# ScalarE's first Silu ahead of its bias loads, in the start of a hybrid attention and convolution layer

## Chip, core and metric

The kernel runs on one core of a Trainium2 chip. The metric is device time in microseconds, the median of several executions. One execution was also taken with the hardware profiler; all rows below are from it.

## What is computed

One layer of a diffusion model with two parallel head groups, in float32. The condition vectors go through Silu and a modulation matrix; the tokens are normalised, scaled and shifted by that, and projected. All the rest (attention, convolution, gates, output) follows from the projections.

```python
mod = jax.nn.silu(c) @ w_mod[l] + b_mod[l]           # c: (1, 1024), w_mod: (1024, 3072)
shift, scale, gate = jnp.split(mod, 3, axis=-1)
mod_c = jax.nn.silu(c_ctx) @ w_mod[l] + b_mod[l]     # the same for the context tokens
u = rms_norm(h, norm_w[l]) * (1.0 + scale[:, None, :]) + shift[:, None, :]   # h: (1, 1024, 1024)
p = u @ w_in[l]                                      # q, k, v, gates, GLU input
...
out = jnp.concatenate([attn, conv], axis=-1) @ w_out[l]
h = h + gate[:, None, :] * out
```

The small vectors that the change moves are `b_mod`, `norm_w`, `conv_b`, `conv_ln_w`, `conv_ln_b` and `b_pw`: together 40 rows of 128 numbers, 20 KB.

## The kernel before

The kernel has three stages: a start and the projections, the attention with the convolution beside it, and the output. Only the start matters here. Most operands of matmuls are split into a rounded high part and a remainder (`split`, L110 to L117), and products are taken of the parts.

`setup` (L139) comes first. It loads the two condition vectors as 16 rows of 128 into `crow` (half by SP, half by ACT) and the six bias vectors as 40 rows into `brow` (all by ACT, L147 to L150). GpSimd makes the identity matrix. TensorE turns `crow` into columns (`pc`, L160), ScalarE takes Silu of that (`sc`, L162), which needs a table load first. TensorE turns `brow` into columns too (`pb`, L169), and VectorE copies these to `bcol` and `vcol` (L171 to L175).

`start` (L949) then runs the steps listed in the string `START`, whose beginning is

```python
"L0 X0 L1 Q0 C0 W0 X1 Q1 L2 Y D0 Q2 R2 R0 L3 L4 Q3 R3 S0 | R1 C1 P00 P10 U00 W1 Q5 D1 M00 ..."
```

- `L` j (`mod_load`, L236): SP loads 256 columns of `w_mod` in four loads of 256 KB, two for each of two tiles; `wm` for j up to 2 (four buffers of the pool `e5`), `wm3s` and on after that.
- `X` h (`load_tokens`, L318): SP loads four token tiles of 512 KB.
- `Q` i (`norm_stats`, L326): ScalarE squares token tile i and sums, VectorE and GpSimd make the factor `rs`. `R` i (`scale`, L968) applies it to the tile on VectorE.
- `C` j (`mod_mm`, L256): TensorE multiplies `sc` with block j of `w_mod` (L265, tile `mrow`). For the first three blocks that is 8 products of full float32, which the trace shows as 16 matmuls.
- `D` j (`mod_cols`, L269): the result is copied out (`mrs`), turned into columns (`mcol`), and `bcol` is added (`modc`).
- `W` h, `S` h: SP loads half of the first projection weight (`wglu0s`), ScalarE and VectorE split it.
- `P` (`turn_x`, L341): transposes of the tokens (`xt`). `U` (`make_u`, L347): ScalarE applies `modc`. `M` (L965): the projection's matmuls (L387).

What sets the order: each engine executes its own queue in order, and a queue of loads is part of the engine that issues them (SP or ACT). The steps ahead of the bar in `START` keep the order written (`manual_schedule`). Everything else in `setup`, `start` and `project` is placed by a planner at build time: by priority in the order of the source, among the instructions that its own model of time has ready. It may put later work into gaps, also between hand-ordered steps. All semaphores are placed by the planner's framework. From the attention on, the order is written by hand again.

Of the kernel before, what the change touches and what calls it, by code (L numbers as in the profile page):

```python
# [12 lines left out]
AF = mybir.ActivationFunctionType  # L13
# [5 lines left out]
P = 128  # L19
# [62 lines left out]
class Layer:  # L82
# [56 lines left out]
    def setup(self):  # L139

        nc, a, cst = self.nc, self.a, self.cst
        row = lambda ap, n: ap.rearrange("o (r f) -> (o r) f", f=P)[0:n]
        crow = self.w2([16, P], "crow")
        brow = self.w2([40, P], "brow")
        nc.sync.dma_start(out=crow[0:8], in_=row(a["c"], 8))
        nc.scalar.dma_start(out=crow[8:16], in_=a["c_ctx"].rearrange("(r f) -> r f", f=P))
        nc.scalar.dma_start(out=brow[0:16], in_=row(a["b_mod"], 16))  # L147
        nc.scalar.dma_start(out=brow[16:24], in_=row(a["norm_w"], 8))
        for i, n in enumerate(("conv_b", "conv_ln_w", "conv_ln_b", "b_pw")):
            nc.scalar.dma_start(out=brow[24 + 4 * i:28 + 4 * i], in_=row(a[n], 4))  # L150
        self.ident = ident = cst.tile([P, P], F32, name="ident")
        make_identity(nc, ident)
        self.identr = cst.tile([P, P], F32R, name="identr")
        nc.vector.tensor_copy(out=self.identr, in_=ident)
        self.mhalf = cst.tile([P, 16], F32, name="mhalf")
        nc.gpsimd.memset(self.mhalf, -0.5)
        self.ones = cst.tile([P, P], F32, name="ones")
        nc.gpsimd.memset(self.ones, 1.0)
        pc = self.bank("t", "pc")
        nc.tensor.transpose(out=pc[:, 0:16], in_=crow, identity=ident[0:16, 0:16])  # L160
        self.sc = sc = cst.tile([P, 16], F32, name="sc")
        nc.scalar.activation(sc, pc[:, 0:16], AF.Silu)  # L162
        self.chl = chl = cst.tile([P, NK, 4], F32R, name="chl")
        cv = chl.rearrange("p k (s w) -> p w s k", w=2)
        scv = sc.rearrange("p (s k) -> p s k", s=2)
        nc.vector.tensor_copy(out=cv[:, 0], in_=scv)
        nc.vector.tensor_sub(out=cv[:, 1], in0=scv, in1=cv[:, 0].bitcast(F32))
        pb = self.bank("t", "pb")
        nc.tensor.transpose(out=pb[:, 0:40], in_=brow, identity=ident[0:40, 0:40])  # L169
        self.bcol = bcol = cst.tile([P, 24], F32, name="bcol")  # L170
        nc.vector.tensor_copy(out=bcol[:, 0:8], in_=pb[:, 0:8])  # L171
        nc.vector.tensor_scalar(out=bcol[:, 8:16], in0=pb[:, 8:16], scalar1=1.0, scalar2=None, op0=ALU.add)
        nc.vector.tensor_copy(out=bcol[:, 16:24], in_=pb[:, 16:24])
        self.vcol = cst.tile([P, 16], F32, name="vcol")
        nc.vector.tensor_copy(out=self.vcol, in_=pb[:, 24:40])  # L175
        self.modc = cst.tile([P, NK, 4], F32, name="modc")
# [897 lines left out]
```

## Time and profile before

| | us |
|---|---|
| median of 3 runs (675.5 to 676.73) | 676.3 |
| the profiled execution | 675.49 |
| its span on the core | 673.7 |
| around the span | 1.8 |

Busy time in the span: PE (matmuls) 646.5 us, 96%; DVE (VectorE) 518.5, 77%; ACT (ScalarE) 350.1, 52%; POOL (GpSimd) 347.7, 52%. The page cuts the span into 40 slices of 16.8 us: PE is busy for 4 tenths of the first, 8 of the second and 9 or more of nearly all that follow; the DMA engines are at 8 tenths and then 9 or more in the first three, and lower after that. So the first 50 us differ from the rest, and the change lies in the first 6.

How to read the rows: times are microseconds from the start of the span. In a timeline a row is start, duration, engine, line, operation, output and inputs, and in brackets the engine's idle time before it and what ended that. SPq and ACTq are the queues on which SP and ACT issue loads; an issue's duration there isn't the transfer's. Releasers are inferred from semaphores; where a wait is put down to something long done, it was another. Ends of matmuls are modelled.

### The profile page before, as it was taken

Reading aid. Unit: us, or ns where it says so; the run is one execution under the profiler, and the core shown is the slowest. Engines: PE = TensorE matmul, PEld = TensorE weight load, DVE = VectorE, ACT = ScalarE, POOL = GpSimd, SP = SyncE. Lnnn points to the kernel's source line nnn. Section 1 sums busy time; section 2 is a strip of 40 time slices with the busy share of each in tenths; the row PEclk is TensorE's granted clock in tenths of the full one; section 3 lists DMA queues with packets and bytes.
Section 4 is the critical chain, followed back from the end, with each engine's and each line's share of the span. In section 5 each row is a group of like instructions: output and inputs, shape, how many; then the busy total and the mean of one; then the engine's idle time right before and its main releaser. Section 6 shows DMA issues by size and latency. Waiting matters only on the chain.

```text
span 673.7 us, 11083 instructions
## 1 busy us (share of the span) xinstructions
PE 646.5 (96%) x4258; PEld 572.8 (85%) x4258; DVE 518.5 (77%) x828; ACT 350.1 (52%) x578; POOL 347.7 (52%) x305
## 2 busy tenths in 40 slices
PE   4899999999999999998999999999999999998997
PEld 1467799888888999998899999999999888987885
DVE  2698789959999999976888888888899856555322
ACT  3564325546343122134888888888888836431000
POOL 1243813966509343796575676887787854211100
PEclk9899999999999999999999999999999999999999
DMA  8994320312652314010010001001100022125611
GB/s 267 315 239 122 101 61 1 95 31 63 218 188 95 94 63 126 1 32 1 1 33 1 1 32 33 32 14 51 32 1 1 1 94 77 64 79 175 231 48 47
DMA packets 51253, 53.29 MB, mean 79 GB/s; under 512 B 4522, under 2 KB 41698, under 8 KB 51201
## 3 DMA queue, kind: packets, MB, share of 16 engines
q1 hardware_dynamic: 51104, 52.57, 25.1%
q8 instruction: 33, 0.54, 0.3%
q14 instruction: 20, 0.16, 0.1%
q10 hardware_dynamic: 96, 0.02, 0.0%
HBM read 44.20 MB, written 8.39 MB: 78 GB/s over the span
## 4 chain that ended last, share of the span: by engine, by line
PE 76%; DVE 15%; DMA 3%; issue 2%; ACT 2%; SPq 1%; DVEq 0%; ACTq 0%
PE o L824 13%; PE pv L719 11%; PE s L641 10%; PE pt L686 10%; DVE y L457 6%; PE g L387 6%; PE a L387 6%; PE kv L413 4%; DVE yp L457 4%; PE q L413 4%; PE zc L387 3%; PE pw L534 3%; PE mrow L265 1%; DMA wm3s<-in_w_mod 1%; DMA wglu0s<-in_w_in 1%
## 5 line engine op out<-in xcount | busy, mean ns | idle before, releaser
L710 POOL TENSOR_TENSOR p<-raw,p 128x512 fp32r<-128x512 f32 x96 | 128.1, 1349 | 64.0 <-DVE p L704 42.2
L641 PE MATMUL s<-kT,qT 128*128 128x512 f32 (+1 forms) x384 | 100.7, 372 | 3.4 <-ACT e L676 3.4
L719 PE MATMUL pv<-p,v 128*128 128x256 f32 x640 | 103.4, 292 | 0.4 <-DVE mm L751 0.2
L457 DVE SCALAR_TENSOR_TENSOR yp<-up,cw,yp 128x1024 f32<-128x1024 f32 x77 | 99.1, 1286 | 1.9
L686 PE MATMUL pt<-ident,e 128*128 128x128 f32 x640 | 93.4, 273 | 0.4 <-ACT raw L695 0.4
L719 PEld LDWEIGHTS pv<-p,v 128*128 128x128 f32 x640 | 86.0, 189 | 4.5 <-DVE mm L751 1.1
L676 ACT ACTIVATE e<-s,nm 128x1280 f32<-128x1280 f32 x64 | 84.9, 1326 | 2.9 <-DVE mj L666 2.9
L659 DVE TENSOR_REDUCE nm<-s 128x1 f32<-128x1024 f32 x64 | 78.0, 1219 | 5.6 <-PE s L641 4.9
L686 PEld LDWEIGHTS pt<-ident,e 128*128 128x128 f32 x640 | 73.5, 141 | 1.5 <-ACT raw L695 1.0
L641 PEld LDWEIGHTS s<-kT,qT 128*128 128x128 f32 x384 | 62.7, 189 | 9.8 <-ACT e L676 3.9
L695 ACT ACTIVATE raw<-pt 128x512 f32<-128x512 f32 x96 | 57.3, 598 | 12.6 <-PE pt L686 8.6
L666 DVE TENSOR_SCALAR_CACHE_REDUCE mj<-s,nm 128x256 bf16<-128x256 f32 x64 | 30.9, 483 | 20.2 <-PE s L641 18.2
L702 ACT ACTIVATE p<-pt 128x512 fp32r<-128x512 f32 x64 | 38.5, 601 | 12.7 <-PE pt L686 11.2
L704 DVE CAST p<-raw 128x512 fp32r<-128x512 f32 x96 | 41.7, 460 | 1.7 <-ACT raw L695 1.2
L710 DVE TENSOR_TENSOR p<-pt,p 128x512 fp32r<-128x512 f32 x64 | 41.2, 681 | 1.6 <-ACT p L702 1.6
L457 DVE SCALAR_TENSOR_TENSOR y<-up,cw,y 128x1024 f32<-128x1024 f32 x25 | 40.7, 1630 | 0.8
L837 DVE TENSOR_TENSOR r<-o,gb 128x512 f32<-128x512 f32 (+1 forms) x17 | 10.8, 655 | 36.1 <-PE o L824 36.1
L442 POOL TENSOR_TENSOR yz<-yz,ct 128x512 f32<-128x512 f32 x24 | 33.1, 1421 | 0.0
L124 POOL TENSOR_TENSOR qr<-qr,mhalf 128x8 f32<-128x8 f32 (+1 forms) x13 | 21.6, 1660 | 7.8 <-DVE qr L123 7.6
L117 POOL TENSOR_TENSOR ul<-u,uh 128x512 fp32r<-128x512 f32 x8 | 12.2, 1528 | 20.8 <-DVE uh L115 14.2
L441 ACT ACTIVATE ct<-up,cw 128x512 f32<-128x512 f32 x24 | 15.7, 714 | 12.8 <-DVE up L425 9.9
L625 ACT ACTIVATE za<-za 128x512 f32<-128x512 f32 x8 | 4.8, 596 | 29.1 <-PE za L413 29.1
(578 smaller groups left out, 1758.4 us busy)
## 6 DMA issues: line engine op xcount, KB each, us to landing
x<-in_x SPq DMA_DIRECT2D x8, 512.0 KB, 5.7
wg<-in_w_mod SPq DMA_DIRECT2D x8, 512.0 KB, 4.2
xr<-in_x SPq DMA_DIRECT2D x8, 512.0 KB, 6.1
out<-r SPq DMA_DIRECT2D x15, 256.0 KB, 2.0
wm<-in_w_mod SPq DMA_DIRECT2D x12, 256.0 KB, 6.6
zc_d<-zc SPq DMA_DIRECT2D x4, 512.0 KB, 3.3
za_d<-za SPq DMA_DIRECT2D x4, 512.0 KB, 4.0
zar<-za_d SPq DMA_DIRECT2D x4, 512.0 KB
```

The source lines that it names most:

```text
L387: nc.tensor.matmul(acc[h], lhsT=ww, rhs=uu[k][:, h * 512:(h + 1) * 512], start=first and i == 0, stop=last and i == 2)
L413: self.nc.tensor.matmul(acc[:, t * 256:(t + 1) * 256], lhsT=x, rhs=y, start=k == 0 and i == 0, stop=k == NK - 1 and i == 2)
L457: nc.vector.scalar_tensor_tensor(out=out, in0=up[:, w:w + S], scalar=cw[:, w:w + 1], in1=y if w else st["y2"], op0=ALU.mult, op1=ALU.add)
L641: mm = nc.tensor.matmul(self.s5[:, s0 + k0:s0 + k0 + n], lhsT=qt[:, h % 4, t * P:(t + 1) * P], rhs=kT[:, w, k0:k0 + n], start=w == 0, stop ...
L659: r = self.nc.vector.reduce_max(out=nm[:, 0:1], in_=self.s5[:, 1536 * t:1536 * t + 1024], axis=AX.X, negate=True)
L676: ex = nc.scalar.activation(e, self.s5[:, t * KEYS:(t + 1) * KEYS], AF.Exp, bias=st["nm", t][:, 1:2], accum_out=st["z"][:, t:t + 1])
L686: nc.tensor.transpose(out=tp[:, i * 256 + t * P:i * 256 + (t + 1) * P], in_=st["e", t][:, (2 * k + i) * P:(2 * k + i + 1) * P], identity=s ...
L695: self.nc.scalar.activation(raw, st["T", k], AF.Copy)
L704: nc.vector.tensor_copy(out=st["p", k][:, 0], in_=st["T", k])
L710: eng.tensor_sub(out=p[:, 1], in0=st["T", k], in1=p[:, 0].bitcast(F32))
L719: nc.tensor.matmul(st["pv"][:, 0:256], lhsT=self.v[:, kt, u[1] // 4].rearrange("p w d -> p (w d)"), rhs=st["p", k][:, j, i * 256:(i + 1) * ...
L824: self.nc.tensor.matmul(o, lhsT=p, rhs=q, start=half == k == i == 0, stop=half == 1 and k == 3 and i == 2)
```

## The change

In `setup`, ScalarE now takes Silu of a column of ones before anything else that it computes, and Silu of the condition vectors after that. The six loads of bias rows, which ACT issued first, stand in the source behind that second Silu. The result of the first Silu isn't used.

```diff
         nc.sync.dma_start(out=crow[0:8], in_=row(a["c"], 8))
         nc.scalar.dma_start(out=crow[8:16], in_=a["c_ctx"].rearrange("(r f) -> r f", f=P))
-        nc.scalar.dma_start(out=brow[0:16], in_=row(a["b_mod"], 16))
-        nc.scalar.dma_start(out=brow[16:24], in_=row(a["norm_w"], 8))
-        for i, n in enumerate(("conv_b", "conv_ln_w", "conv_ln_b", "b_pw")):
-            nc.scalar.dma_start(out=brow[24 + 4 * i:28 + 4 * i], in_=row(a[n], 4))
+        one = self.small([P, 1], "sj", "sj")
+        nc.vector.memset(one, 1.0)
+        nc.scalar.activation(one, one, AF.Silu)
         self.ident = ident = cst.tile([P, P], F32, name="ident")
...
         nc.scalar.activation(sc, pc[:, 0:16], AF.Silu)
+        nc.scalar.dma_start(out=brow[0:16], in_=row(a["b_mod"], 16))
+        nc.scalar.dma_start(out=brow[16:24], in_=row(a["norm_w"], 8))
+        for i, n in enumerate(("conv_b", "conv_ln_w", "conv_ln_b", "b_pw")):
+            nc.scalar.dma_start(out=brow[24 + 4 * i:28 + 4 * i], in_=row(a[n], 4))
```

## Rows read from the trace of the kernel before

**Rows 1.** The page, chain that ended last: shares of the span by engine.
```profile
PE 76%; DVE 15%; DMA 3%; issue 2%; ACT 2%; SPq 1%; DVEq 0%; ACTq 0%
```

**Rows 2.** The same chain in its first 36 us: start, duration, what.
```profile
1.20 3.13 DMA wm<-in_w_mod
...
4.34 5.50 DMA x<-in_x
...
11.30 6.95 DMA wglu0s<-in_w_in
...
24.21 7.19 DMA wm3s<-in_w_mod
...
31.42 1.07 ACT wm30h L113
...
34.39 2.14 DVE wm31l L117
```

**Rows 3.** Timeline of ACT and its queue, 0 to 20 us.
```profile
1.35 0.33 ACTq L147 DMA_DIRECT2D brow<-in_b_mod  x1
...
2.56 0.26 ACTq L150 DMA_DIRECT2D brow<-in_conv_ln_w  x1
3.75 0.26 ACTq L150 DMA_DIRECT2D brow<-in_conv_ln_b  x1
...
4.59 1.28 ACT L162 ACT_TABLE_LOAD   x1 [4.59 <-DMA brow<-in_norm_w]
5.88 0.18 ACT L162 ACTIVATE sc<-pc 128x16 f32<-128x16 f32 x1
9.87 1.06 ACT L330 ACTIVATE junk<-x 128x1024 bf16<-128x1024 f32 x1 [3.81 <-DMA x<-in_x]
...
13.81 1.06 ACT L330 ACTIVATE junk<-x 128x1024 bf16<-128x1024 f32 x1 [0.23 <-DMA x<-in_x]
```

**Rows 4.** Timeline of PE, 0 to 30 us.
```profile
2.67 0.25 PE L160 MATMUL pc<-ident,crow 16*128 16x16 f32 x1 [2.67 <-DMA crow<-in_c]
6.12 5.56 PE L265 MATMUL mrow<-wm,sc 128*2 128x256 f32 x16 [3.19 <-ACT sc L162]
11.61 0.25 PE L169 MATMUL pb<-ident,brow 40*128 40x40 f32 x1
...
15.72 5.30 PE L265 MATMUL mrow<-wm,sc 128*2 128x256 f32 x16 [0.84 <-DMA wm<-in_w_mod]
20.95 1.09 PE L344 MATMUL xt<-ident,x 128*128 128x128 f32 x8
...
26.22 3.66 PE L265 MATMUL mrow<-wm,sc 128*2 128x256 f32 x16 [0.95 <-DMA wm<-in_w_mod]
```

**Rows 5.** Waits of SP's queue, 4 to 6 us (sum, times, longest), and its second x issue.
```profile
SPq L322 <- DMA wm<-in_w_mod: 1.6, 2, 1.1
...
5.19 0.34 SPq L322 DMA_DIRECT2D x<-in_x  x1
```

**Rows 6.** Windows: busy us by engine (instructions), granted clock, DMA share, GB/s.
```profile
2.00:3.00 1.00, 0.25 (x1) 0.18 (x1) 0.00 (x0) 0.00 (x0) 0.00 (x0) 1.00 0.34 90
6.00:7.00 1.00, 0.88 (x3) 0.29 (x4) 0.37 (x2) 0.06 (x1) 0.00 (x0) 1.00 0.78 262
9.00:9.50 0.50, 0.50 (x3) 0.14 (x2) 0.00 (x0) 0.00 (x0) 0.00 (x0) 1.00 0.65 238
14.00:31.00 17.00, 13.85 (x61) 6.64 (x62) 10.77 (x28) 7.62 (x13) 4.52 (x14) 0.90 1.11 317
```

**Rows 7.** Timeline of DVE, 0 to 24 us.
```profile
1.49 0.23 DVE L154 CAST identr<-ident 128x128 fp32r<-128x128 f32 x1 [1.49 <-POOL ident masks.py:199]
...
13.17 0.75 DVE L969 TENSOR_SCALAR x<-x,rs 128x1024 f32<-128x1024 f32 x1 [0.67 <-POOL rs L124]
13.84 0.16 DVE L171 COPY bcol<-pb 128x8 f32<-128x8 f32 x1
...
18.92 0.75 DVE L969 TENSOR_SCALAR x<-x,rs 128x1024 f32<-128x1024 f32 x1 [1.40 <-POOL rs L124]
```

## Prediction

> **What bounds the kernel now.** I read the engine shares of the chain that ended last first: PE holds 76% of it, DVE 15%, DMA 3% [rows 1]. The change touches only the first microseconds, so the question is what leads there. The same chain, cut to its first 36 us, answers it: up to 31.40 us it runs through loads and SP's issues of them (wm, x, wglu0s, wm3s), then through ACT's and DVE's splits of wm3s [rows 2]. ACT's Silu of the condition vectors (`sc`) and the first group of modulation matmuls behind it (L265; "C0" below) are not on it. Next I read ACT in order of time [rows 3]: a load of `crow`, six loads of the bias rows `brow` from 1.35 to about 4.55 us, the table load (1.28 us), then `sc`, 5.88 to 6.06 us. Then PE [rows 4]: the transpose `pc` that feeds `sc` was done at 2.92 us, so `sc` was late by some 3 us for ACT's own queue, and C0 began with `sc`, at 6.12. Last the DMA share of windows [rows 6]: from 14 to 31 us it is above 1.0, which is full; in the first 9.5 us there are holes. So the start is paced by bytes, and what the change can win is what it makes those bytes start earlier, not what it makes ScalarE start earlier.
>
> **The change part by part.**
>
> *The constant Silu.* Added: a memset of one column (DVE is idle until 1.49 us [rows 7]) and a Silu of one column. The nearest row for its price is `sc` itself, 0.18 us [rows 3]. The table load does not wait for an operand: it can start where the first bias load was issued, 1.35 us, and ends at 1.35 + 1.28 = 2.63, the constant Silu at 2.81. `pc` ends at 2.92. Cost: nothing, since ACT would wait for `pc` anyway; if `pc` came at once, it would be 0.18.
>
> *`sc` earlier.* It could run at 2.95 to 3.15, some 2.9 us earlier. C0 can't use this whole: its first operand tile is filled by the first two loads of wm. The first landed at 4.33 [rows 2]; the second x issue, at 5.19, ends a wait on SP for the second [rows 5]. C0 then starts at 5.2 in place of 6.12: 0.95 us earlier, and ends near 10.7 instead of 11.68 (5.56 us long [rows 4]; its second operand tile is in by then or holds it up by a few tenths). Who uses that? `pb` stands behind C0 on PE and could move to 10.7, but its readers on DVE (`bcol`, 13.84) stand behind a scaling of x at 13.17, which waits for POOL and, through it, for x [rows 7]. The second group of matmuls (15.72) waits for a load of wm [rows 4]. So of the 0.95 us I carry 0.
>
> *The bias loads later.* Six issues move from 1.35 behind `sc`. Each took 0.26 to 0.33 us [rows 3], so they would go out from about 3.2 to 5.4 us if nothing held them, about 1 to 2 us later than now. Before, the last was issued just ahead of the table load, at some 4.3, and none held up `pb`, which ran at 11.61, as soon as C0 was through. Even 4 us later they land before `bcol` could run. Cost 0, with that slack as cover; without it a microsecond late is a microsecond on `bcol`, then on the 0.9 us of slack that x's scaling has ahead of the transposes (18.92 + 0.75 = 19.67 [rows 7] against 20.95 [rows 4]).
>
> *The order of issue on the two queues.* This is the term that counts. SP's issues of x wait for landings of wm: 1.1 and 0.5 us for the first two [rows 5]. The first x load waits for the first wm load, the second for the second, and nothing in the kernel's text asks for that. Counting both queues in their order of issue, the one waited for stands eight places ahead each time. I read from this that a load may go out only when the one eight places before has landed. Now six of the first sixteen places are bias loads. If these go behind, the first x load has `crow` or nothing ahead of it and goes out at 3.3 in place of 4.34. What that is worth is bounded by the unused DMA time of this stretch [rows 6]: 1 - 0.34 = 0.66 us in 2 to 3, 0.22 in 6 to 7, 0.5 x 0.35 = 0.17 in 9 to 9.5, together 1.05 us. The lower bound is 0. I take 0.22 + 0.17 and a fifth of the 0.66 (most of that is the loads' own run-up after their issue at 1.20, but bias packets also run in it): 0.5 us. From 14 to 31 us the share is 1.11 [rows 6], so a gain goes on to the landing of wm3s undiminished; from there ACT and DVE follow directly [rows 2].
>
> *The clock.* PE is idle for longer between C0 and the second group. From 14 to 31 us the granted clock is 0.90 on average [rows 6], so for a part at the lower of its two levels; the second group took 5.30 us, the third 3.66 [rows 4]. Wholly at the lower level it would take about 2 x 3.66 = 7.3, so 2.0 more; the third group has 0.95 us of idle time ahead of it [rows 4], which leaves 0 to +1.05. I take 0, as the group already was slow for most of its time.
>
> Sum: 0 + 0 + 0 - 0.5 + 0 = -0.5 us, between -1.05 and +1.05. The profiled execution took 675.49 (span 673.7, 1.8 around it), so 675.0; the median of the runs stands 0.8 above it, so 676.3 - 0.5 = 675.8.
>
> **The rivals.**
>
> *Nothing moves.* Outside the hand-written stretch a planner puts instructions on an engine as they become ready: the scaling of x at 13.17 comes later in the source than the `bcol` copies that it runs ahead of [rows 7]. The bias loads are ready at once, `sc` only at 2.9 us: the planner may put them ahead of `sc` all the same, and the change then doesn't do what it says. With six issues of 0.26 to 0.33 us and the gaps between them after the constant Silu, `sc` ends near 5 to 6 us. Time 676.3, within 0.4. The Trainium skill comes to no gain by another way (DMA: Bandwidth & Descriptors, "Issuing engines are not separate DMA queues"): the choice of issuing engine saves only the sequencer's time, which it calls usually small beside the transfer. Here ACT's sequencer was taken from 1.35 to 4.59 us by 20 KB of bias rows [rows 3], which speaks against "small"; that bytes keep the pace of the start speaks for the rule. By it the time is 676.3.
>
> *ScalarE is held behind its own loads.* By the eight-places reading a bias load placed behind x loads waits for one of them to land, and ScalarE executes in order: the four squares of x (9.87 to some 15.0 [rows 3]) are queued behind it. If the last bias load is held to the landing of the fourth x tile (13.8 [rows 3]), the squares end near 13.8 + 0.3 + 5.1 = 19.2, x's last scaling near 21: just about at the transposes of 20.95, so little is lost. If it is held by a later load, wglu0s (landing 18.25 [rows 2]), they end at 23.7, the transposes start near 25.5, 4.5 us late, of which PE's idle time up to 32.5 (some 2 us) hides part: +2.5 to +3. It decides from a hold past about 14 us. Time 679. For it: a tiny load, the fifth of the bias rows, already went out 0.93 us after the issue before it was done [rows 3]. Against it: SP issues one load in about 0.5 us, so by 3 us it has placed only some five, and the bias loads come soon after.
>
> *The order of later work falls otherwise.* The planner orders everything up to the attention by its own times, and these move by a microsecond. One split on DVE, which leads after 32 us, is 1 to 2.1 us [rows 2]; one swap is about 1.8 us either way: 674.5 or 678.1.
>
> **How the numbers follow.** About 0.2% (1.35 us) is what a measurement of this kernel can tell from no change. Forecast 0.48, its own range 675.0 to 676.4 (the median itself moves by 0.6), of which 0.10 is beyond 0.2% faster. Nothing moves 0.16, all of it within 0.2%. ScalarE held 0.14, of which 0.12 slower and 0.02 within. Another order later 0.22: 0.10 faster, 0.10 slower, 0.02 within. So faster 0.20, same 0.38 + 0.16 + 0.02 + 0.02 = 0.58, slower 0.22. The range leaves out the far ends of the last two: 674.5 to 678.6.
>
> **What would show it.** Right: the table load near 1.35 us, `sc` near 3, C0 at about 5.2 and led by a load of wm, the first x issue near 3.3, a fuller DMA in 6 to 7 us, the landing of wm3s some 0.5 us earlier. Wrong: bias loads ahead of `sc` on ACT (the first rival); squares of x that start later than 9.9 with ACT's issues waiting before them (the second); wm3s earlier, but PE's first long busy stretch not (the third). It would also be wrong if C0's earlier end were handed on, that is if `bcol` moved with `pb`.

## The result, and the profile after

| | before | after |
|---|---|---|
| median, us | 675.76 (675.36 to 676.73, 6 runs) | 679.74 (678.48 to 681.68, 6 runs) |
| profiled execution / its span, us | 675.49 / 673.7 | 678.48 / 676.7 |

The changed kernel is slower: ratio 1.0054, 95% interval 1.0038 to 1.0070. The forecast was 675.8, its range ended at 678.6, and slower by over 0.2% had a chance of 0.22. Below, each kernel's median stands beside that of the kernel before on the same chip (it differs between chips, 676.03 to 677.63); behind them in brackets are the ratio and its 95% interval. Ratios leave out one execution of 2260.07 us, of `third_group_first`, far beyond all others.

ScalarE did what the change says. Timeline of ACT and its queue in the kernel after (start, duration, engine, what, idle time before it), against [rows 3]:

```profile
1.34 1.28 ACT L149 ACT_TABLE_LOAD   x1 [1.34 <-PEq L1064]
1.40 0.33 ACTq L162 DMA_DIRECT2D brow<-in_b_mod  x1
...
2.63 0.20 ACT L149 ACTIVATE sj<-sj 128x1 f32<-128x1 f32 x1
2.95 0.18 ACT L161 ACTIVATE sc<-pc 128x16 f32<-128x16 f32 x1
2.96 0.25 ACTq L165 DMA_DIRECT2D brow<-in_conv_b  x1
...
4.45 0.26 ACTq L165 DMA_DIRECT2D brow<-in_b_pw  x1
9.35 1.06 ACT L333 ACTIVATE junk<-x 128x1024 bf16<-128x1024 f32 x1 [6.22 <-DMA x<-in_x]
```

The table load went from 4.59 to 1.34 us, `sc` from 5.88 to 2.95. The planner left two of the six bias loads ahead of `sc` (the first is shown) and put four behind. No engine's work waited for any of them.

What it brought and what it cost, on PE, against [rows 4]:

```profile
5.16 5.66 PE L268 MATMUL mrow<-wm,sc 128*2 128x256 f32 x16 [2.25 <-DMA wm<-in_w_mod]
...
15.63 5.30 PE L268 MATMUL mrow<-wm,sc 128*2 128x256 f32 x16 [1.55 <-DMA wm<-in_w_mod]
20.87 1.09 PE L347 MATMUL xt<-ident,x 128*128 128x128 f32 x8
...
26.18 3.37 PE L268 MATMUL mrow<-wm,sc 128*2 128x256 f32 x8 [2.80 <-DMA wm<-in_w_mod]
29.48 0.65 PE L390 MATMUL g<-uh,wglu00h 128*128 128x512 f32 x1
...
31.20 1.89 PE L268 MATMUL mrow<-wm,sc 128*2 128x256 f32 x8
```

The first group starts at 5.16 instead of 6.12, and at the second group (15.63, before 15.72) and the transposes (20.87, before 20.95) that is gone. Up to 21 us the kernels are level. Then the order differs. The first half of the third group stands ahead of the first GLU matmuls ("M00"), and these, though ready, wait behind it: PE is idle for 2.80 us until `wm20` has landed. This is the same part of the kernel before:

```profile
23.60 0.50 PE L387 MATMUL g<-uh,wglu00h 128*128 128x512 f32 x1
...
24.87 0.40 PE L387 MATMUL a<-uh,wglu00l 128*128 128x512 f32 x1
```

There M00 ran at 23.60, inside the wait for `wm20` (26.22, [rows 4]). In the kernel after it starts at 29.48. The half that PE waited for was slow as well: 3.37 us for 8 matmuls, where the second half took 1.89. The windows of PE's granted clock (columns as in [rows 6]) say why:

```profile
14.00:31.00 17.00, 12.11 (x46) 5.18 (x44) 8.23 (x20) 7.99 (x14) 4.29 (x12) 0.80 1.13 323
...
22.00:26.40 4.40, 1.05 (x8) 0.62 (x9) 2.68 (x8) 4.40 (x8) 1.49 (x2) 1.00 1.18 309
26.42:29.80 3.38, 3.38 (x9) 1.03 (x8) 0.58 (x3) 1.07 (x3) 0.19 (x3) 0.50 1.15 274
```

Some 0.2 us after PE's idle time ended the clock is at the lower of its two levels (0.50), and stays there for the whole of this half. From 14 to 31 us it is 0.80 on average; before it was 0.90 [rows 6].

Of the other steps that stand elsewhere in the order of after, two stand out. On POOL the memsets of `up`, which wait for that half, stand ahead of the last two factors `rs`; on DVE the scaling of `wq`, which waits for a small load, stands ahead of the split `wm31l`. POOL and DVE of the kernel after:

```profile
29.61 0.11 POOL L423 MEMSET up<- 128x15 f32 x1 [3.59 <-PE mrow L268]
...
29.72 1.38 POOL L124 TENSOR_TENSOR rs<-rs,mhalf 128x1 f32<-128x1 f32 x2
30.31 1.58 DVE L972 TENSOR_SCALAR x<-x,rs 128x1024 f32<-128x1024 f32 x2 [3.30 <-POOL rs L124]
...
36.19 0.19 DVE L206 TENSOR_SCALAR wq<-wq 128x64 f32<-128x64 f32 x1
36.29 1.22 DVE L117 TENSOR_TENSOR wm31l<-wm3s,wm31h 128x1024 fp32r<-128x1024 f32 x1
```

The same on DVE before:

```profile
34.31 2.22 DVE L117 TENSOR_TENSOR wm31l<-wm3s,wm31h 128x1024 fp32r<-128x1024 f32 x1
36.45 0.41 DVE L115 CAST uh<-u 128x512 fp32r<-128x512 f32 x1
36.79 0.27 DVE L191 COPY cw<-pcw 128x124 f32<-128x124 f32 x1
36.98 1.30 DVE L203 TENSOR_SCALAR wq<-wq 128x64 f32<-128x64 f32 x1
```

How much is lost by when? The first Sigmoid of the GLU closes this stretch. Timeline of ACT, before and then after:

```profile
71.02 1.09 ACT L424 ACTIVATE sg<-g 128x512 f32<-128x512 f32 x2
```
```profile
73.75 1.09 ACT L427 ACTIVATE sg<-g 128x512 f32<-128x512 f32 x2
```

It comes 2.73 us later, of the 3.0 us between the spans; from there to the end it is 602.7 and 602.9 us. So the loss lies between 21 and 71 us. PE in this stretch, before and then after (start and end, length, busy us, clock, DMA share, GB/s):

```profile
20.95:71.02 50.07, 45.66 (x274) 1.00 0.81 216
```
```profile
20.87:73.75 52.88, 47.59 (x274) 0.97 0.74 200
```

The same 274 matmuls keep PE busy for 1.93 us longer, and it is idle for 0.88 us longer.

I call the start of ACT's row "the Sigmoid" and give it beside each median. It is read from one execution of each kernel. Of the 18 profiled executions told of here, 11 have further stretches at the lower clock near 320 or 617 us; those of the kernel before and of the changed one have none. Such stretches can spread the medians, and the Sigmoid comes ahead of them.

### The profile page after: what moved, and what is told of

It is laid out like the page before. It is cut to its first block, busy times and chain, and to the rows that moved or that the text cites. A ratio compares the mean times of both kernels' runs of the same rounds, so it can differ in the third digit from the quotient of the medians.

```text
span 676.7 us, 11086 instructions
## 1 busy us (share of the span) xinstructions
PE 648.8 (96%) x4258; PEld 573.1 (85%) x4258; DVE 516.9 (76%) x829; ACT 350.3 (52%) x579; POOL 348.2 (51%) x305
## 4 chain that ended last, share of the span: by engine, by line
PE 73%; DVE 16%; issue 3%; SPq 3%; DMA 2%; ACT 1%; POOL 1%; DVEq 0%; ACTq 0%; POOLq 0%
PE o L827 13%; PE pv L722 11%; PE s L644 10%; PE pt L689 9%; DVE y L460 6%; PE g L390 6%; PE a L390 6%; PE kv L416 4%; DVE yp L460 4%; PE q L416 4%; PE zc L390 3%; PE pw L537 3%; DMA wm<-in_w_mod 2%; SPq L219 2%; PE mrow L268 1%
## 5 line engine op out<-in xcount | busy, mean ns | idle before, releaser
L707 DVE CAST p<-raw 128x512 fp32r<-128x512 f32 x96 | 43.8, 482 | 1.7 <-ACT raw L698 1.2
L705 ACT ACTIVATE p<-pt 128x512 fp32r<-128x512 f32 x64 | 38.5, 602 | 12.5 <-PE pt L689 11.0
L355 ACT ACTIVATE u<-xt,modc 128x512 f32<-128x512 f32 x16 | 12.2, 775 | 21.0 <-PE xt L347 16.5
L268 PE MATMUL mrow<-wm,sc 128*2 128x256 f32 x48 | 16.2, 509 | 6.6 <-DMA wm<-in_w_mod 6.6
```

What stands on the lines that cost most here:

```text
L707: nc.vector.tensor_copy(out=st["p", k][:, 0], in_=st["T", k])
```

## The experiments

Kernels whose order is given by hand have this method, called at the end of the build. PIN lists the instructions of PE, DVE, POOL and ACT by number, in the order wanted; the method chains each to the one before it, without semaphores, and leaves out those in the range HAND. In the cuts of PIN below, instructions are written by line and tile in place of their numbers.

```diff
+    def pin(self):
+        edge = mybir.DependencyInfo(mybir.DependencyClass.NoSync, mybir.DependencyReason.DATA)
+        for chain in PIN:
+            names = [f"I-{n}" for n in chain.split()]
+            for a, b in zip(names, names[1:]):
+                if not int(b[2:]) in HAND:
+                    self.tc.add_manual_dep(self.nc.find_inst_by_name(b), a, edge, reason="order")
```

### Is it the edit, or the order that the planner makes of it?

`edit_old_order`: the whole change, with PIN set to the order of the kernel before.

> The whole change, but with the order of the kernel before written out by hand on PE, POOL, DVE and ACT for the start (ScalarE's first ten instructions excepted, which are those of the change). Theory (the loss is the planner's other order of the steps behind the start; the change itself is harmless): near or below the kernel before, 674.8 to 676.0, first group of L265 at about 5.2 us and the first projection matmul (L387 before) at about 23.5. Rival (the change costs by itself: later bias rows, or ScalarE's front): still 679 to 680.

`no_edit_new_order`: the kernel before, with PIN set to the order of the kernel after.

> The kernel before in all its instructions, with the order of the changed kernel written out by hand on PE, POOL, DVE and ACT for the start. Theory (the order is the loss): slower than before by 3 to 4.5 us, 679 to 680.5, with PE idle for some 2.8 us ahead of the third group of L265 and two factors on POOL held to some 29.5 us. Rival (the change itself costs): 675.5 to 676.5.

Measured: the change in the old order took 677.37 against 677.63 (0.9998, 0.9984 to 1.0013), Sigmoid 71.45. The kernel before in the new order took 680.77 (1.0058, 1.0037 to 1.0079), Sigmoid 74.31. The edit itself costs nothing that can be told; the order is the loss.

### Which part of the edit changes the order?

`silu_first_loads_next`: the constant Silu alone; the loads stay where they were.

```diff
+        one = self.small([P, 1], "sj", "sj")
+        nc.vector.memset(one, 1.0)
+        nc.scalar.activation(one, one, AF.Silu)
         nc.scalar.dma_start(out=brow[0:16], in_=row(a["b_mod"], 16))
```

> The constant Silu first, but the bias loads in the source right behind it and ahead of everything else: the planner then makes the order of the kernel before on PE, POOL, DVE and SP. It shows what an earlier table load is worth alone. By the start's pace (loads): first group of L265 about 0.9 us earlier, time 675.2 to 676.3, no difference or up to 0.5 us gained. If the constant Silu were the cost: 678 or more.

`loads_behind_alone`: the six loads behind `sc`, no constant Silu.

```diff
-        nc.scalar.dma_start(out=brow[0:16], in_=row(a["b_mod"], 16))
...
         nc.scalar.activation(sc, pc[:, 0:16], AF.Silu)
+        nc.scalar.dma_start(out=brow[0:16], in_=row(a["b_mod"], 16))
...
```

> The bias loads behind the Silu of the condition vectors, without the constant Silu: the planner makes the order of the changed kernel. Theory (order): 679 to 680.5, like the changed kernel, though its table load comes later by a bit. If the constant Silu were needed for the loss: 675.5 to 676.5.

Measured: the Silu alone 678.02 against 677.63 (1.0007, 0.9993 to 1.0022), Sigmoid 71.15, and PE, DVE and POOL keep the old order. The loads alone 680.84 (1.0056, 1.0036 to 1.0076), Sigmoid 74.08, with the order of after on PE and POOL. The planner answers to the place of the loads. Which of its modelled times tips was not tried.

### Which step of the new order costs the time?

First the two that the traces show best: PE's third group and POOL's memsets.

`third_group_first`: the kernel before in its own order, but with the first half of the third group (L265 on `wm20`) ahead of M00 (L387).

```diff
-L387 g a g g a a; L265 wm20; L265 wm21
+L265 wm20; L387 g a g g a a; L265 wm21
```

> The kernel before, with one thing moved: the first half of the third group of modulation matmuls (8 of 16, on wm20) is put ahead of the first six GLU matmuls on PE; all else keeps its order, the memsets of up behind all eight factors rs too. Milestone: the first Sigmoid of the GLU, at 71.0 to 71.5 us where the old order was run, at 73.8 to 74.3 where the new order was. Theory A (PE idles until wm20 has landed at some 26.2 us, with ready GLU matmuls queued behind the waiting one): PE idle about 2.8 us there, first GLU matmul at 27.9 to 29.5, Sigmoid at 73.2 to 74.3, time 2.5 to 4 us above before. Theory B (the loss came by POOL: memsets that wait for this half, ahead of the last two factors rs): Sigmoid at 71.0 to 71.6, time within 0.2% of before. If both share it, the Sigmoid lies near 72.3.

`memsets_first_alone`: the kernel before, with POOL's order of after alone.

```diff
-L124 rs; L124 rs; L420 up; L421 up
+L420 up; L421 up; L124 rs; L124 rs
```

> The kernel before, with POOL's order of after alone: the memsets of up stand ahead of the last two factors rs; PE keeps the old order. The half of the third group that the memsets wait for ends at about 28.0 to 28.5 us here, so rs comes some 0.3 to 0.6 us later than the 27.95 us of the old order and x's last scalings with it. Theory A (PE's order alone): Sigmoid at 71.0 to 71.6, time within 0.2% of before. Theory B (POOL's order alone): Sigmoid at 73 or later. A late rs that counts as it is: Sigmoid 0.3 to 0.6 us later, which the time can't tell.

`after_memsets_last`: the kernel after, where the memsets follow all eight factors (`behind` adds an order without a semaphore).

```diff
-        nc.gpsimd.memset(up[:, 0:PAD], 0.0)
-        nc.gpsimd.memset(up[:, S + PAD:S + 2 * PAD], 0.0)
+        for o in (0, S + PAD):
+            ms = nc.gpsimd.memset(up[:, o:o + PAD], 0.0)
+            if b >= 2:
+                self.behind(ms, self.pows[:8])
```

> The kernel after, with its memsets of up (second batch of buffers) put behind all eight factors rs on POOL; PE keeps the new order, the first half of the third group ahead of the GLU matmuls. Theory A (PE's order alone): rs back at 27.1 to 28.0 us, but the Sigmoid stays at 73.2 to 74.3 and the time 2.5 to 4 us above before. Theory B (POOL's order alone): Sigmoid at 71.0 to 71.6 and a time within 0.2% of before. In between, near 72.3: each has a part.

Measured: the memsets cost nothing that can be told. Alone they give 676.32 against 677.19 (0.9996, 0.9981 to 1.0011), Sigmoid 71.66; put back they bring `rs` to 28.02 and the Sigmoid stays at 74.66 (680.71, 1.0052, 1.0032 to 1.0072). The third group alone costs 1.9 us: Sigmoid 72.95, 678.88 (1.0022, 1.0007 to 1.0036). On PE it shows the two rows of after again:

```profile
26.47 3.37 PE L302 MATMUL mrow<-wm,sc 128*2 128x256 f32 x8 [2.59 <-DMA wm<-in_w_mod]
29.77 0.64 PE L424 MATMUL g<-uh,wglu00h 128*128 128x512 f32 x1
```

But 1.9 is less than I had expected (2.2 to 3.3), and less than the 2.7 to 3.3 of the new order as a whole. Something else costs too.

### The second step: a scaling that waits for its load

`scale_first_alone`: the kernel before in its own order, but with the scaling of `wq` ahead of `wm31l` on DVE.

```diff
-L117 wm31l; L115 uh; L191 cw; L203 wq
+L203 wq; L117 wm31l; L115 uh; L191 cw
```

> The kernel before with one thing moved on DVE: the scaling of wq (it waits for a small load that SP issues at about 32.1 us) stands ahead of the split wm31l, as in the order of after, in place of three instructions behind it. The third group keeps its old place. Theory C (the third group's place carries the whole loss): Sigmoid at 71.0 to 71.6 us, as in the old order. Theory D (the two have a part each): wq's load lands at some 36.3 us, wm31l ends at 37.6 to 38.4 in place of 36.5 to 36.9, PE idles 1.0 to 1.8 us ahead of the matmuls that read it, Sigmoid at 72.0 to 72.9 and the time 0.8 to 1.8 us above before.

`rest_of_order`: as `no_edit_new_order`, but with the third group whole and behind M00, and POOL's order as before.

```diff
-L265 wm20; L387 g a g g a a; L265 wm21
+L387 g a g g a a; L265 wm20; L265 wm21
...
-L420 up; L421 up; L124 rs; L124 rs
+L124 rs; L124 rs; L420 up; L421 up
```

> The kernel before in the order of after on PE, DVE and ACT, but with the first half of the third group back behind the first six GLU matmuls, and the memsets of up behind the factors rs. Theory C (the third group's place carries the whole loss): Sigmoid at 71.0 to 71.7 us, time within 0.2% of before. Theory D (wq's scaling ahead of wm31l has a part of its own): wm31l ends at 37.6 to 38.4, PE idle 1.5 to 2.5 us ahead of its matmuls, Sigmoid at 72.4 to 73.2, time 1.3 to 2.5 us above before.

`scale_first_load_early`: `scale_first_alone`, with the load of `wq` issued ahead of `wm3s`.

```diff
+        self.tc.add_manual_dep(self.wq_load.ins, self.cw_load.ins.name, edge, reason="order")
+        self.tc.add_manual_dep(self.wm3_load.ins, self.wq_load.ins.name, edge, reason="order")
```

> The same as scale_first_alone (wq's scaling ahead of wm31l on DVE, Sigmoid 73.91), but wq's load is issued ahead of the loads of wm3s in place of behind those of wm4s, so that it has landed long before the scaling: this takes away what the scaling waits for, and leaves its place. Theory D (the loss is the wait for that load, with DVE's splits queued behind): scaling at about 34.5 to 35 us, wm31l done by 36.9, Sigmoid at 71.0 to 71.9 (up to 0.4 for the load ahead of wm3s), time within 0.2% of before. If the place itself costs, the Sigmoid stays at 73 or later.

Measured: the scaling alone costs 2.9 us (Sigmoid 73.91; 679.21 against 676.03, 1.0039, 1.0024 to 1.0055). The rest of the order, without the third group's place, costs the whole loss and more (74.75, where 72.4 to 73.2 was expected; 681.09, 1.0069, 1.0052 to 1.0087). With the load early the loss is gone (71.81; 677.59 against 677.33, 1.0000, 0.9989 to 1.0012). DVE of `scale_first_alone`, then PE, then its windows:

```profile
36.39 0.20 DVE L240 TENSOR_SCALAR wq<-wq 128x64 f32<-128x64 f32 x1 [2.02 <-DMA wq<-in_q_norm_w]
36.50 1.22 DVE L145 TENSOR_TENSOR wm31l<-wm3s,wm31h 128x1024 fp32r<-128x1024 f32 x1
```
```profile
37.78 0.28 PE L302 MATMUL mrow<-wm31l,chl 128*4 128x256 f32 x1 [0.95 <-DVE wm31l L145]
```
```profile
49.80:52.50 2.70, 1.24 (x6) 0.68 (x5) 2.67 (x7) 1.39 (x2) 0.11 (x1) 1.00 0.00 0
53.10:56.50 3.40, 3.40 (x19) 2.43 (x17) 3.16 (x7) 0.27 (x1) 1.48 (x1) 0.50 0.02 5
```

DVE stands idle for 2.02 us until the load has landed, with the ready split `wm31l` behind it. PE waits 0.95 us for that split and comes to it 1.12 us later than before:

```profile
36.66 0.28 PE L265 MATMUL mrow<-wm31l,chl 128*4 128x256 f32 x1
```

This much was expected. The remaining 1.8 us were not: a stretch at the lower clock from 53.1 to 56.5 us, which the kernel before does not have. Why it came there is not shown: PE idled for 0.67 and 0.79 us shortly ahead of it, but in the kernel before 1.59 us of idle time ahead of the same matmuls brought none. And of `scale_first_load_early` the rows on DVE:

```profile
34.91 1.20 DVE L242 TENSOR_SCALAR wq<-wq 128x64 f32<-128x64 f32 x1
36.03 1.21 DVE L145 TENSOR_TENSOR wm31l<-wm3s,wm31h 128x1024 fp32r<-128x1024 f32 x1
```

The scaling stands in the same place, waits for nothing, and costs nothing that can be told. It is the wait, not the place.

### How the two stand together in the changed kernel

`after_third_group_behind`: the kernel after with one rule; the planner orders the rest.

```diff
+                if j == 2:
+                    self.behind(mm, self.m00)
```

> The kernel after with one ordering rule added: the third group of modulation matmuls stands behind the first six GLU matmuls on PE. The planner is left to order the rest, and with this it also puts wm31l ahead of wq's scaling again. Theory D (the place of the group and that of wq are the loss): first GLU matmul at 23.5 to 24.9 us, wm31l done by 37.2, Sigmoid at 71.0 to 71.9, time within 0.2% of before. If something else of the new order cost the time, or the early Silu itself, the Sigmoid stays beyond 72.5 and the time 2 us or more above before.

`after_idle_filled`: the kernel after in its order, with PE's idle time ahead of the third group filled.

```diff
+        if j == 2:
+            for _ in range(FILL):
+                nc.tensor.matmul(rows[0:2, 0:P], lhsT=scv[:, :, 0], rhs=self.ident, start=True, stop=True)
```

> The kernel after in its own order, with 11 more matmuls (2x128, on data long there; their result is overwritten) put on PE into the 2.80 us in which it waits for wm20, ahead of the first half of the third group. The wait stays, only its idle time is filled. Theory K (the low granted clock of that half, 3.37 us in place of some 1.8, is a part of the loss): if the clock is then granted in full, the half ends near 28.1, the first GLU matmul starts at 28.0 to 28.3 in place of 29.48, and the Sigmoid comes 1.2 to 1.6 us sooner, at 72.1 to 72.6. Theory L (the split wm31l, held by wq's load to 37.6 to 38.4 us, takes it back): the first GLU matmul at 28.0 to 28.3, but PE idles 1 to 1.8 us ahead of the matmuls on wm31l, and the Sigmoid stays at 73.2 to 73.9. If the clock falls all the same, nothing changes: 73.75.

`after_scale_behind`: the kernel after in its order, with the scaling of `wq` put back. `after_both_undone`: that (the first two lines below), and the third group whole behind M00. `after_again`: the kernel after, unchanged, beside these.

```diff
-L206 wq; L117 wm31l; L115 uh; L194 cw
+L117 wm31l; L115 uh; L194 cw; L206 wq
...
-L268 wm20; L390 g a g g a a; L268 wm21
+L390 g a g g a a; L268 wm20; L268 wm21
```

> The kernel after in its own order, with wq's scaling alone put back behind wm31l; the third group keeps its new place. If each of the two is enough by itself, most of the loss stays: Sigmoid at 72.7 to 73.8, as in the run of the old order with the third group alone moved (72.95). If wq's place is the whole loss: 71.0 to 71.7.

> The kernel after in its own order, POOL's memsets of up included, but with two things put back: the first half of the third group behind the first six GLU matmuls on PE, and wq's scaling on DVE behind wm31l and the two copies that follow it. Theory D (these two places are the loss, either of them by itself enough for most of it): first GLU matmul at 23 to 25 us, wm31l done by 37.0, Sigmoid at 71.0 to 71.7, time within 0.2% of before. If a third thing of the new order costs time, the Sigmoid stays at 72.5 or later.

> The kernel after, unchanged, on the chip of these runs, as the measure for the three others: Sigmoid at 73.7 to 74.5, time 0.4 to 0.7% above before.

Measured, against 677.33: both undone 677.98 (1.0016, 1.0001 to 1.0031), Sigmoid 71.90; the scaling alone undone 680.13 (1.0052, 1.0027 to 1.0077), Sigmoid 75.41 (72.7 to 73.8 was expected; that execution was some 1.2 us late at 17 us already, by its loads); after itself 679.03 (1.0037, 1.0021 to 1.0054), Sigmoid 74.08. So either step by itself is enough for most of the loss, and only without both is most of it gone.

The filled kernel shows why the two don't add up. PE, its clock, and DVE:

```profile
23.14 2.56 PE L307 MATMUL mrow<-ident,sc 128*2 128x128 f32 x22
26.19 1.89 PE L310 MATMUL mrow<-wm,sc 128*2 128x256 f32 x8 [0.49 <-DMA wm<-in_w_mod]
28.01 0.50 PE L432 MATMUL g<-uh,wglu00h 128*128 128x512 f32 x1
...
38.26 0.28 PE L310 MATMUL mrow<-wm31l,chl 128*4 128x256 f32 x1 [1.97 <-DVE wm31l L147]
```
```profile
26.10:29.80 3.70, 3.61 (x15) 1.76 (x16) 1.63 (x5) 1.22 (x3) 1.48 (x4) 1.00 1.14 283
36.30:38.20 1.90, 0.00 (x0) 0.00 (x0) 1.33 (x3) 1.48 (x2) 0.00 (x0) 1.00 0.96 286
39.30:42.60 3.30, 3.30 (x11) 2.63 (x10) 3.30 (x4) 0.00 (x0) 0.60 (x1) 0.50 1.19 290
```
```profile
36.87 0.19 DVE L245 TENSOR_SCALAR wq<-wq 128x64 f32<-128x64 f32 x1 [2.21 <-DMA wq<-in_q_norm_w]
36.98 1.22 DVE L147 TENSOR_TENSOR wm31l<-wm3s,wm31h 128x1024 fp32r<-128x1024 f32 x1
```

With the idle time filled the clock stayed up, the half took 1.89 us instead of 3.37, and M00 came 1.5 us sooner. PE then stood 1.97 us for `wm31l`, held by `wq`'s load, and the lower clock came 13 us later instead (39.3 to 42.6). Sigmoid 74.70, 681.20 against 676.03 (1.0065, 1.0043 to 1.0088): nothing was won. Two other kernels of the new order show the same with nothing filled in: in `no_edit_new_order` and `after_memsets_last` the half took 1.89 us at the full clock after idle times of 1.57 and 1.85, PE then waited 1.54 and 1.76 us for `wm31l`, and the lower clock came at 38.5 and 38.2. In the kernel after PE is so late by the third group that `wq`'s load has landed when DVE comes to it (no wait at 36.19). Whoever mends one step meets the other.

`after_third_group_behind` met it in another place, and my expectation was wrong: M00 ran at 23.16 and `wm31l` was done by 35.57, but the planner now put the scaling ahead of the `uh` that PE needs next, DVE waited 1.10 us for the same load, and a stretch of 6.8 us at the lower clock (39.35 to 46.17) followed. Sigmoid 76.28, 681.00 (1.0061, 1.0044 to 1.0078).

### The prediction's own term

`loads_all_behind_old_order`: the whole change in the old order, all six loads held behind `sc`, as the prediction took it.

```diff
+        for d in loads:
+            self.tc.add_manual_dep(d.ins, first.ins.name, edge, reason="order")
```

> The whole change with all six bias loads held behind the Silu of the condition vectors, and the later steps pinned to the old order: this is the change as the prediction took it, and tries its term of -0.5 us by itself. If a load waits for the landing of the one eight places before, the first two x loads now have eight places of c, c_ctx, wm only in front and go out at 3.3 and 3.8 us in place of 4.34 and 5.19. Theory of the prediction: the DMA share from 6 to 7 us rises from 0.78 to near 1.0, wm3s lands 0.2 to 1 us earlier, Sigmoid at 70.2 to 70.9, time 0.2 to 1.0 us below the whole change in the old order. Rival (the bytes come earlier but PE's own work up to 70 us, at the clock granted, sets the pace): x lands earlier, Sigmoid at 71.0 to 71.5, no difference in time. Second rival (ScalarE held behind its own loads): the squares of x begin 1 us or more later than 9.9, Sigmoid at 72 or later.

Measured: 675.85 against 677.19 (0.9991, 0.9977 to 1.0005), Sigmoid 71.22. The issues of x, the second and third group, and SP's waits from 9 to 32 us:

```profile
3.31 0.50 SPq L365 DMA_DIRECT2D x<-in_x  x1
```
```profile
4.16 0.34 SPq L365 DMA_DIRECT2D x<-in_x  x1
```
```profile
15.30 6.17 PE L308 MATMUL mrow<-wm,sc 128*2 128x256 f32 x16 [0.79 <-DMA wm<-in_w_mod]
25.82 3.66 PE L308 MATMUL mrow<-wm,sc 128*2 128x256 f32 x16
```
```profile
SPq L291 <- PE mrow L308: 1.0, 1, 1.0
```

The first x load goes out at 3.31, as worked out. The second waits until 4.16, not to 3.8 as I expected of this run: two bias loads still take places among the loads of wm. The bytes do come earlier, by 0.42 and 0.40 us at the second and third group [rows 4]. The DMA share from 6 to 7 us was 0.87, not near 1.0. Then SP waits 1.0 us, which it does not before, for PE's second group to free a buffer of `wm`, and `wm30h` starts at 31.40, level with [rows 2]. The group itself was slower here, 6.17 us against 5.30, at a clock of 0.53 on average (columns as in [rows 6]):

```profile
14.00:21.00 7.00, 6.07 (x17) 2.10 (x18) 3.90 (x9) 1.58 (x3) 1.25 (x4) 0.53 1.13 350
```

So the expectation's first rival, that PE at the clock granted sets the pace, describes this trace: it had the Sigmoid at 71.0 to 71.5. That the edit brought the lower clock here is not shown: the second group took 3.70 us in `memsets_first_alone` and 6.44 in `no_edit_new_order`, and neither has the edit.

### All of them

| kernel | half of third group ahead of M00 | `wq` scaled, unlanded, ahead of needed work | Sigmoid | ratio to before |
|---|---|---|---|---|
| before | no | no | 71.02 | 1 |
| edit_old_order | no | no | 71.45 | 0.9998 |
| silu_first_loads_next | no | no | 71.15 | 1.0007 |
| loads_all_behind_old_order | no | no | 71.22 | 0.9991 |
| memsets_first_alone | no | no | 71.66 | 0.9996 |
| scale_first_load_early | no | no | 71.81 | 1.0000 |
| after_both_undone | no | no | 71.90 | 1.0016 |
| third_group_first | yes | no | 72.95 | 1.0022 |
| after_scale_behind | yes | no | 75.41 | 1.0052 |
| scale_first_alone | no | yes | 73.91 | 1.0039 |
| rest_of_order | no | yes | 74.75 | 1.0069 |
| after_third_group_behind | no | yes | 76.28 | 1.0061 |
| after, after_again | yes | yes, landed by then | 73.75, 74.08 | 1.0054, 1.0037 |
| loads_behind_alone | yes | yes | 74.08 | 1.0056 |
| no_edit_new_order | yes | yes | 74.31 | 1.0058 |
| after_memsets_last | yes | yes | 74.66 | 1.0052 |
| after_idle_filled | yes | yes | 74.70 | 1.0065 |

Every kernel with neither has its Sigmoid below 72 us, every one with either beyond 72.9. The spread among the first (71.02 to 71.90) is not explained in full; `memsets_first_alone` and `scale_first_load_early` have a stretch at the lower clock in their third group (from 27.5 and 27.4 to 30.9 and 30.8 us), but a second group of 3.70 us. No version was faster than the kernel before by more than its interval.

## Why the prediction was wrong

*The constant Silu: 0.* Right. It ran at 2.63, ahead of `pc`'s end, and alone it is worth nothing (1.0007).

*`sc` earlier: 0.* Right to 0.04 us (2.95; first group 5.16 against 5.2), and led by a load of wm. What I had named as a sign of an error came true, though: `bcol` moved with `pb`, from 13.84 to 11.05, as the planner put it ahead of x's scaling. Nothing was handed on even so, since the second group waited for its load.

*The bias loads later: 0.* Right: the last went out at 4.45, and `bcol` had all by 11.05.

*The order of issue: -0.5.* Half right in mechanism, and not shown in the time. In the changed kernel two bias loads kept their places ahead of `sc`, the others went out from 2.96 to 4.45 us, around the first load of x, and x still waited for wm (4.18, before 4.34). So the first rival, that the planner leaves bias loads ahead of `sc`, described this part. The eight places are right in another count than the one given: by start times the first two x loads of the kernel before stand ten and nine places behind the loads that they waited for. In the trace loads use eight semaphores in turn, in the planner's order, and each waits for the load that had its semaphore before. Where all six went behind, the first x load went out at 3.31, as this has it, and the bytes were 0.4 us early until the third group. "A gain goes on to the landing of wm3s undiminished" is the sentence that fell: SP's 1.0 us of wait for a buffer, behind a second group of 6.17 us, took it back in that trace. The time can't tell: its interval (0.9991, 0.9977 to 1.0005) holds 0 and also the -0.5 of the forecast. By the rule of the Trainium skill weighed there (DMA: Bandwidth & Descriptors, "Issuing engines are not separate DMA queues") the edit would have come to no gain, and in the old order none can be told: 0.9998.

*The clock: 0, at most +1.05.* Wrong in place for the changed kernel. I had priced a slower second group; that took 5.30 us in both kernels. The cost came in the third group, by 3.37 - 1.89 = 1.5 us, behind the 2.80 us of idle time that the new order put there. In the run of the term by itself the second group was slower, by 0.87, inside what I had priced.

*ScalarE held behind its loads.* Did not happen: the squares began at 9.35, before 9.87.

*The order of later work.* This was the cause, and this is the step that failed. The sum had no term for it, only the range. It had a chance of 0.22, split evenly between both signs, and a price of 1.8 us, one split on DVE. The price was taken from the duration of a moved instruction. What the swap cost here is what the moved instruction *waits for* while ready work stands behind it: 2.80 us on PE for `wm20`, less the 0.95 [rows 4], 0.41 and 0.39 us that PE idled between 25 and 33 us before and no longer does, so 1.05. PE before:

```profile
32.53 0.28 PE L265 MATMUL mrow<-wm30h,chl 128*4 128x256 f32 x1 [0.41 <-ACT wm30h L113]
33.20 0.66 PE L344 MATMUL xt<-ident,x 128*128 128x128 f32 x4 [0.39 <-ACT u L352]
```

With the 1.5 us of lower clock that is 2.5 of the 2.73. So more than half of the loss came through the lower clock, which the rival's price did not hold. The swap of `wq`, by itself, cost 2.9, of which the wait was 1.12 and the stretch at the lower clock the rest. The rows for both prices were in the trace of before: the end of the wait for `wm20` (26.22) with M00 inside it, and `wq`, whose load was issued at 32.08 and which was scaled at 36.98, with DVE's splits around it. The even split of signs is not borne out: in the order of before these two waits were covered, and a swap that takes the cover away can only lose. That no other order gains is not shown.

What stays open: why moving the loads tips the planner, which idle times bring a stretch at the lower clock, and the last 0.16% of `after_both_undone` (interval from 0.01%), which no run told apart.

## What to carry to other kernels

Where a planner orders the work, an edit at the start is also an edit of everything that it orders behind: pin the old order and run the edit in it, and the two effects separate in one run. To price a change of order, look for instructions that wait long for a load, list what stands ready behind them on their engine, and take the wait, less the idle time that it replaces, not the instruction's duration. Here a stretch at the lower clock behind each wait cost more than the wait itself. A small load that is asked for late can be brought forward cheaply; here that took away the cost of one swap (1.0000), while mending the one place that the trace showed only uncovered the next.

## What the runs showed of the hardware

Lower clock after idle time, but not after each: in the kernel after PE idled 2.80 us and its clock was at 0.50 from 0.24 us after that; with the idle time filled it stayed at 1.00 there, and fell 1 us after the next idle time, of 1.97. The 0.95 us of idle time in `scale_first_alone` brought no lower clock near it, and neither did 1.57 and 1.85 us in `no_edit_new_order` and `after_memsets_last`, ahead of the same half. A stretch cost 1.5 to 1.8 us of a busy PE in the kernel after and in `scale_first_alone`, more than either wait added by itself (1.05 and 1.12).

In `scale_first_alone` a load of 32 KB took 4.3 us from its issue to its use: `wq`, issued at 32.07 behind four loads of 256 KB, was scaled at 36.39, as soon as it had landed. And DVE's time for the same instruction changes by what POOL does beside it: `wm31l` took 2.22 us in the kernel before, beside a subtraction on POOL (34.15 to 35.44), and 1.22 in `scale_first_alone`, where POOL's was over. So part of the 2.02 us of wait came back at once: the split ended only 1.2 us later (37.72 against 36.53). The Trainium skill (SBUF — State Buffer, "SBUF: two separate sides") says that VectorE and GpSimd share one pair of ports, and that a VectorE instruction with two inputs in SBUF and a GpSimd one that reads SBUF hold it in turn, each alone for its whole instruction. The two rows are of this kind, and the 1.00 us more, where they overlap by 1.13, agrees. POOL's row beside `wm31l`, in the kernel before:

```profile
34.15 1.29 POOL L117 TENSOR_TENSOR ul<-u,uh 128x512 fp32r<-128x512 f32 x1 [4.05 <-DVE uh L115]
```
